# Retention in pairs of heads, and block squares added on GpSimd, in a two-layer backbone kernel

## The chip, the core and the metric

The kernel runs on one core of a Trainium2 chip. The metric is device time in microseconds (us) of one execution. The core has TensorE (matmuls into PSUM banks), VectorE, ScalarE, GpSimd and the queue of SyncE, which issues the transfers from HBM. Each engine works through its own instructions in order, and semaphores make it wait for the others.

## What is computed

Two layers act on a context of 256 tokens and an input of 256 tokens, 1024 channels each. Layer 0 mixes neighbourhood attention with a state-space scan (16 heads of 64, 2 groups) and has a dense feed-forward part; layer 1 mixes sliding-window attention with retention (8 heads) and has a mixture of eight experts. The two parts that matter here:

```python
# state space: gate, then a root-mean-square norm over each group of 512 channels
yz = (y * jax.nn.silu(z)).reshape(b, L, SSM_GROUPS, SSM_D_INNER // SSM_GROUPS)
yz = yz * lax.rsqrt(jnp.mean(jnp.square(yz), axis=-1, keepdims=True) + EPS)

# retention: decayed linear attention in both directions, then a layer norm per head
rf_c, rf_l = scan_from_context(rv_c, ga_c[0], rk_c, rq_c, rv_l, ga_l[0], rk_l, rq_l, False, need_ctx)
rb_c, rb_l = scan_from_context(rv_c, ga_c[1], rk_c, rq_c, rv_l, ga_l[1], rk_l, rq_l, True, need_ctx)
yr_l = jax.nn.silu(rgl) * head_layernorm(rf_l + rb_l, gn_g, gn_b)
```

Query and key of a retention head have 64 channels (`RET_QK_DIM`), its value 128. All arithmetic is fp32; large projections are split into a high and a low part and done as three matmuls.

## The kernel before, in words

Activations lie with channels on the 128 partitions and tokens along the row. The kernel is written stage by stage in Python; a planner takes the instructions, their dependencies and the buffers they need, and lays down for each engine an order in which an instruction written earlier goes first if it is ready. So the order of work around a line is mostly the order of the program, but whatever isn't ready in the plan is overtaken by what is written behind it. A buffer or PSUM bank is taken from a named tag; a tag has a fixed number of them ("ax", "pt" and "mm" two banks each, "po" and "ada" one; "Pm" two tiles of 128x512), and a new one waits until the old one's readers are done.

State-space stage (`ssm2`, L854 to L917). A loop goes over eight blocks `pr` of 128 channels, four to each norm group. For each block, two directions and two heads, TensorE spreads a row of decays (L877), ScalarE or VectorE turns it into a masked tile E (L882, L885, L887, L888), GpSimd scales the inputs to `xd` for three of the four combinations (L893), and TensorE multiplies (L898; the two heads go to the lower and upper 64 output partitions) and adds the off-diagonal part (L901). VectorE multiplies with the gate (L903), ScalarE squares the result into a "Pm" tile (L909), and `gsum` (L836) lets TensorE sum the squares over the partitions: four matmuls a block with a column of ones, one for each 128 tokens, all four blocks of a group into one bank. The squares of a block are summed one block later. `gdiag` and `gnorm` then build the norm. Between the blocks the output projection `out_proj` (L930) is woven in.

Retention stage (`ret`, L1213 to L1254). A loop goes over eight heads `h`. Two heads share a tile: an even head has partitions 0 to 63 of `rkT`, `rqT`, `Q` and `Hr`, an odd one 64 to 127 (`rr`). Per head: two score matmuls with 64 rows (L1220) into an "ax" bank, a multiply with the decay on VectorE (L1224), two state matmuls with 64 rows (L1228) and two with the values (L1230) into a second "ax" bank, then the layer norm: a copy (L1232), a matmul with ones for the mean (L1233), its subtraction (L1234), squares on ScalarE (L1236) and their sum by `T.matmul` with a column of ones (L1238). After heads 3 and 7 the norm of four heads is finished (L1243 to L1254) and split into `yH`, `yL`. One step of `ret` is taken after each of eight gate projections (L1257 to L1262); the output projections (L1276 and L1307) follow, and the first of them fills TensorE while retention runs. The experts' weights (L1403) are loaded into memory that retention's tiles leave.

Of the kernel before, what the change touches and what calls it, by code (L numbers as in the profile page):

```python
# [13 lines left out]
AF = mybir.ActivationFunctionType  # L14
ALU = mybir.AluOpType
# [3 lines left out]
P = 128  # L19
# [148 lines left out]
def tile_backbone(ctx: ExitStack, tc: tile.TileContext, A, out, upto=99, dbg=None):  # L168
    nc = tc.nc
    V, S, T, G = nc.vector, nc.scalar, nc.tensor, nc.gpsimd  # L170
# [25 lines left out]
    def bank(tag="mm"):  # L196
        if turn and tag == "ax":
            turn.append(turn.pop(0))
            tag = turn[0]
        return ps[0].tile([P, 512], F32, tag=tag, name="bk_" + tag, bufs=NB[tag])  # L200
# [29 lines left out]
    ident, ones = C("ident"), C("ones")  # L230
# [7 lines left out]
    def hp(shape, name, dt=F32):  # L238
        return pool[0].tile(shape, dt, tag="hp", name=name, bufs=NHP)
# [288 lines left out]
    def layer0():  # L528
# [168 lines left out]
        pt = bank("pt")  # L697
# [18 lines left out]
        pst = bank("ax")  # L716
# [13 lines left out]
        for i in range(4):  # L730
            for c in range(4):
                T.matmul(pac[32 * i:32 * i + 32, c * P:(c + 1) * P], av[:, c, :], C("tge" if i % 2 else "tle"),
                         start=True, stop=True, tile_position=(0, 32 * i))
# [10 lines left out]
        for i, m in enumerate((8, 9, 10, 11, 0, 1, 2, 3, 4, 5, 6, 7)):  # L744
# [4 lines left out]
            for d in (-2, -1, 1, 2):  # L749
# [3 lines left out]
                                       op0=ALU.mult, op1=ALU.add)  # L753
# [79 lines left out]

        psq, bks = [], []

        def gsum(pr, sq):  # L836
            for t in range(4):
                T.matmul(bks[pr // 4][:, t:t + 1], sq[:, t * P:(t + 1) * P], ones[:, 0:1],
                         start=pr % 4 == 0 and t == 0, stop=pr % 4 == 3, skip_group_check=True)

        def gdiag(g):
            return diag(rstd(bks[g][:, 0:4], 4, 1.0 / 512), 4)
# [11 lines left out]
        def ssm2():  # L854
            cbf = pg([P, 4, 2, P], "cbf")
            cbb = pg([P, 4, 2, P], "cbb")
            for g in range(2):
                pt = bank("ax")
                for c in range(4):
                    r = slice(c * P, (c + 1) * P)  # L860
                    T.matmul(pt[:, r], BT[:, g, r], CT[:, g, r], start=True, stop=True)
                ptv = pt.rearrange("p (c k) -> p c k", c=4)
                V.tensor_tensor(cbf[:, :, g, :], ptv, C("tle")[:, None, :].to_broadcast([P, 4, P]), op=ALU.mult)
                V.tensor_tensor(cbb[:, :, g, :], ptv, C("tge")[:, None, :].to_broadcast([P, 4, P]), op=ALU.mult)
            yield
            Eb = [pg([P, 2, 4, P], "E") for _ in range(5)]
            for pr in range(8):
                g = pr // 4
                py = bank("pt")
                for d in range(2):  # L870
                    Es = []
                    E2 = Eb[(2 * pr + d) % len(Eb)]
                    for hh in range(2):
                        o = d * 16 + 2 * pr + hh
                        sel = 32 * d + o
                        pt = bank("ax")
                        T.matmul(pt, idr[:, sel:sel + 1].to_broadcast([P, P]), ac2, start=True, stop=True)  # L877
                        E = E2[:, hh]
                        onact = (d, hh) in ONACT
                        for c in range(4):  # L880
                            if onact:
                                S.activation(E[:, c, :], pt[:, c * P:(c + 1) * P], AF.Relu, scale=-1.0,  # L882
                                             bias=acj[:, c, o:o + 1])
                            else:
                                V.tensor_scalar(E[:, c, :], pt[:, c * P:(c + 1) * P], lnda[:, c, o:o + 1],  # L885
                                                lndt[:, c, o:o + 1], op0=ALU.add, op1=ALU.min)
                        S.activation(E, E, AF.Exp, scale=-1.0 if onact else 1.0)  # L887
                        V.tensor_tensor(E, E, (cbb if d else cbf)[:, :, g, :], op=ALU.mult)  # L888
                        xh = [xtok[c][:, (2 * pr + hh) * 64:(2 * pr + hh + 1) * 64] for c in range(4)]
                        if onact:  # L890
                            xd = hp([P, 4, 64], "xd")
                            for c in range(4):
                                G.tensor_scalar(xd[:, c, :], xh[c], dt[:, c, o:o + 1], None, op0=ALU.mult)  # L893
                            xh = [xd[:, c, :] for c in range(4)]
                        Es.append((xh, E))
                    for c in range(4):
                        for hh in range(2):
                            T.matmul(py[hh * 64:hh * 64 + 64, c * P:(c + 1) * P], Es[hh][0][c],  # L898
                                     Es[hh][1][:, c, :], start=d == 0 and c == 0, stop=False, skip_group_check=True)
                for c in range(4):  # L900
                    T.matmul(py[:, c * P:(c + 1) * P], yo[c][:, pr * P:(pr + 1) * P], ident, start=False, stop=True,  # L901
                             skip_group_check=True)
                V.tensor_tensor(z(pr), z(pr), py, op=ALU.mult)  # L903
                if pr % 4 == 0:
                    bks.append(bank("po"))
                if psq:
                    gsum(*psq.pop())
                sq = pm_([P, 512])
                S.activation(sq, z(pr), AF.Square)  # L909
                psq.append((pr, sq))  # L910
                yield
                if pr == 4:
                    dg = gdiag(0)
                if pr == GN0:
                    gnorm(0, dg)
            gsum(*psq.pop())
            gnorm(1, gdiag(1))  # L917

        s1 = ssm1()
# [87 lines left out]
    def layer1(hH, hL):  # L1007
# [39 lines left out]
        rkT = Act(4, "rk")  # L1047
        rqT = pg([P, 4, 256], "rq")
# [21 lines left out]
        for m in range(4):  # L1070
            pp = proj(3 + m, 256)
            q = hp([P, 2, 256], "qtmp")
# [5 lines left out]
        rv = [pg([P, 1024], "rv") for _ in range(4)]  # L1078
# [3 lines left out]
        pt = bank("pt")  # L1082
# [60 lines left out]
        dec = [pg([P, 2, 2, 256], "dec") for _ in range(4)]  # L1143
# [35 lines left out]
        Q = []  # L1179
# [32 lines left out]

        def ret():  # L1213
            pst = bank("ada")
            for h in range(8):
                rr = slice((h % 2) * 64, (h % 2) * 64 + 64)
                t = h // 2
                pa = bank("ax")
                for jt in range(2):
                    T.matmul(pa[:, jt * 256:jt * 256 + 256], rkT(t, 256 + jt * P, 256 + jt * P + P)[rr],  # L1220
                             rqT[rr, t, :], start=True, stop=True)
                e = dec[h // 2][:, h % 2]
                ef = e.rearrange("p a b -> p (a b)")
                V.tensor_tensor(ef, ef, pa, op=ALU.mult)  # L1224
                bk = bank("ax")
                py, pm = bk[:, 0:256], bk[:, 256:512]
                for d in range(2):
                    T.matmul(py, Hr[rr, d, t * P:(t + 1) * P], Q[d][rr, t, :], start=d == 0, stop=False)  # L1228
                for jt in range(2):
                    T.matmul(py, rv[2 + jt][:, h * P:(h + 1) * P], e[:, jt, :], start=False, stop=jt == 1)  # L1230
                yv = yc[h // 4][:, h % 4, :]
                V.tensor_copy(yv, py)  # L1232
                T.matmul(pm, ones, yv, start=True, stop=True)  # L1233
                V.scalar_tensor_tensor(yv, pm, -1.0 / P, yv, op0=ALU.mult, op1=ALU.add)  # L1234
                sq = hp([P, 256], "sqv")
                S.activation(sq, yv, AF.Square)  # L1236
                for q in range(2):
                    T.matmul(pst[:, h * 2 + q:h * 2 + q + 1], sq[:, q * P:(q + 1) * P], ones[:, 0:1],  # L1238
                             start=h == 0 and q == 0, stop=True, skip_group_check=True)
                yield  # L1240
                if h % 4 == 3:
                    g = h // 4
                    r = rstd(pst[:, g * 8:g * 8 + 8], 8, 1.0 / P)  # L1243
                    for q in range(2):
                        pb = bank("ax")
                        diag_bcast(pb, r[:, q * 4:q * 4 + 4], 4)
                        for i in range(2):
                            hh = g * 4 + q * 2 + i
                            yv = yc[g][:, hh % 4, :]
                            V.scalar_tensor_tensor(yv, yv, vc("rgg")[:, hh:hh + 1], pb[:, i * 256:i * 256 + 256],  # L1250
                                                   op0=ALU.mult, op1=ALU.mult)
                            V.scalar_tensor_tensor(yv, yv, vc("rgb")[:, hh:hh + 1], rgs[g][:, hh % 4, :],
                                                   op0=ALU.add, op1=ALU.mult)
                            split(yH[g][:, hh % 4, :], yL[g][:, hh % 4, :], yv)  # L1254
# [681 lines left out]
    with tc.tile_pool(name="pgp", bufs=1) as pgp:  # L1936
# [3 lines left out]
        h = layer0()  # L1940
# [31 lines left out]
```

## Time and profile before

| | us |
|---|---|
| three runs | 2107.56, 2121.23, 2126.02 (median 2121.23) |
| the profiled execution | 2105.75 |
| its span from the first to the last instruction | 2103.9 |
| TensorE busy | 2035.0 |
| VectorE busy | 1284.7 |
| ScalarE busy | 905.3 |
| GpSimd busy | 102.6 |

The profile is of one execution. The busy time of TensorE is modelled for pipelined matmuls, so two matmuls in a row can overlap in it; the distance from one start to the next start is the surer reading of what a matmul costs. "PE" is TensorE's matmuls and "PEld" its weight loads, "DVE" VectorE, "ACT" ScalarE, "POOL" GpSimd, "SPq" SyncE's queue of transfers. A wait is put down to what ended it. An fp32 matmul shows as two TensorE instructions.

### The profile page before, as it was taken

Reading aid. Unit: us, or ns where it says so; the run is one execution under the profiler, and the core shown is the slowest. Engines: PE = TensorE matmul, PEld = TensorE weight load, DVE = VectorE, ACT = ScalarE, POOL = GpSimd, SP = SyncE. Lnnn points to the kernel's source line nnn. Section 1 sums busy time; section 2 is a strip of 40 time slices with the busy share of each in tenths; the row PEclk is TensorE's granted clock in tenths of the full one; section 3 lists DMA queues with packets and bytes.
Section 4 is the critical chain, followed back from the end, with each engine's and each line's share of the span. In section 5 each row is a group of like instructions: output and inputs, shape, how many; then the busy total and the mean of one; then the engine's idle time right before and its main releaser. Section 6 shows DMA issues by size and latency. Waiting matters only on the chain. (4 is left out here: it accounts for less than half of the span.)

```text
span 2103.9 us, 26774 instructions
## 1 busy us (share of the span) xinstructions
PE 2035.0 (97%) x10210; PEld 1444.8 (69%) x10210; DVE 1284.7 (61%) x1878; ACT 905.3 (43%) x1296; POOL 102.6 (5%) x143
## 2 busy tenths in 40 slices
PE   7999999989999999999999999999999999999997
PEld 4776756678777878888888888878654544545453
DVE  5366557677566664775468888898644334434543
ACT  4347515643222223544346766767532232232322
POOL 0000015500000000101101000000000000000000
PEclk9999999999999999999999999999999999999998
DMA  8423432024444673322434999999989999999984
GB/s 322 151 86 104 151 113 92 25 67 161 143 147 150 214 237 120 124 66 78 149 143 170 336 365 326 322 331 337 372 336 400 397 400 397 383 418 384 384 356 179
DMA packets 89445, 496.25 MB, mean 236 GB/s; under 512 B 10080, under 2 KB 10848, under 8 KB 46048
## 3 DMA queue, kind: packets, MB, share of 16 engines
q1 hardware_dynamic: 89312, 494.49, 64.1%
q8 instruction: 82, 1.34, 0.3%
q14 instruction: 51, 0.42, 0.1%
HBM read 493.40 MB, written 1.05 MB: 235 GB/s over the span
## 5 line engine op out<-in xcount | busy, mean ns | idle before, releaser
L270 DVE TENSOR_TENSOR w<-w 128x2048 fp32r<-128x2048 f32 (+1 forms) x186 | 384.6, 2081 | 64.1 <-ACT w L269 46.4
L269 ACT ACTIVATE w<-w 128x2048 fp32r<-128x2048 f32 (+1 forms) x186 | 320.5, 1748 | 67.7 <-DVE w L270 35.5
L269 ACT ACTIVATE whi<-raw 128x1024 fp32r<-128x1024 f32 x151 | 159.8, 1060 | 400.7 <-PE bk_mm L298 270.4
L270 DVE TENSOR_TENSOR wlo<-raw,whi 128x1024 fp32r<-128x1024 f32 x151 | 184.8, 1225 | 136.0 <-ACT whi L269 135.1
L297 PE MATMUL bk_mm<-fH,whi 128*128 128x512 f32 (+1 forms) x360 | 139.8, 390 | 2.0 <-DVE xT L518 1.1
L299 PE MATMUL bk_mm<-fH,wlo 128*128 128x512 f32 (+1 forms) x360 | 138.8, 387 | 2.1 <-DVE wlo L270 2.1
L297 PE MATMUL bk_mm<-hH,whi 128*128 128x512 f32 (+1 forms) x384 | 137.2, 360 | 3.2 <-ACT hH L269 2.2
L298 PE MATMUL bk_mm<-fL,whi 128*128 128x512 f32 (+1 forms) x360 | 139.2, 388 | 0.0
L298 PE MATMUL bk_mm<-hL,whi 128*128 128x512 f32 (+1 forms) x384 | 135.6, 354 | 0.0
L299 PE MATMUL bk_mm<-hH,wlo 128*128 128x512 f32 (+1 forms) x384 | 135.2, 353 | 0.0
L1542 PE MATMUL bk_pt<-w,xf 128*64 128x512 f32 x448 | 113.0, 601 | 0.0
L1695 ACT COPY g<-bk_ax 64x512 f32<-64x512 f32 x35 | 20.4, 582 | 207.9 <-PE bk_ax L1542 207.8
L1542 PE MATMUL bk_ax<-w,xf 128*64 128x512 f32 x448 | 107.2, 597 | 0.0
L1754 PE MATMUL bk_mm<-w,gf 128*64 128x512 f32 x448 | 105.3, 597 | 0.0
L1546 PE MATMUL bk_ax<-w,xg 128*128 128x512 f32 x224 | 91.6, 409 | 9.6 <-DVE w L270 9.6
L1545 PE MATMUL bk_ax<-w,xg 128*128 128x512 f32 x224 | 90.1, 402 | 0.0
L1547 PE MATMUL bk_ax<-w,xg 128*128 128x512 f32 x224 | 89.7, 400 | 0.0
L1546 PE MATMUL bk_pt<-w,xg 128*128 128x512 f32 x220 | 88.1, 400 | 0.4 <-DVE w L270 0.2
L1545 PE MATMUL bk_pt<-w,xg 128*128 128x512 f32 x220 | 87.6, 398 | 0.0
L1547 PE MATMUL bk_pt<-w,xg 128*128 128x512 f32 x220 | 87.3, 397 | 0.0
L297 PEld LDWEIGHTS bk_mm<-hH,whi 128*128 128x128 f32 x384 | 71.7, 188 | 22.2 <-issue 5.4
L456 POOL TENSOR_TENSOR rstd<-rstd,mhalf 128x2 f32<-128x2 f32 (+2 forms) x11 | 10.3, 937 | 1513.9 <-DVE rstd L455 1486.0
(567 smaller groups left out, 4367.4 us busy)
## 6 DMA issues: line engine op xcount, KB each, us to landing
w<-in_m SPq DMA_DIRECT2D x334, 1024.0 KB, 7.9
raw<-in_f SPq DMA_DIRECT2D x66, 512.0 KB, 3.7
araw<-in_adc SPq DMA_DIRECT2D x56, 512.0 KB, 3.9
araw<-in_ada SPq DMA_DIRECT2D x32, 512.0 KB, 7.0
raw<-in_evx SPq DMA_DIRECT2D x29, 512.0 KB, 3.8
raw<-in_odx SPq DMA_DIRECT2D x22, 512.0 KB, 3.7
raw<-in_evo SPq DMA_DIRECT2D x12, 512.0 KB, 3.6
xT<-in_xt SPq DMA_DIRECT2D x4, 1024.0 KB, 6.2
```

Source lines behind the costliest of these rows:

```text
L269: a = S.activation(hi, src, AF.Copy)
L270: v = V.tensor_tensor(lo, src, hi.bitcast(F32), op=ALU.subtract)
L297: T.matmul(o, wh, xh, start=first, stop=False)
L298: T.matmul(o, wh, xl, start=False, stop=False)
L299: T.matmul(o, wl, xh, start=False, stop=last)
L456: G.tensor_tensor(r, r, mhalf[:, :n], op=ALU.pow)
L1542: T.matmul(o[c:c + 64], sl(b[0]), wh, start=k < 2, stop=k >= K - 2, tile_position=(0, c))
L1545: T.matmul(o, sl(b[0]), wh, start=first, stop=False)
L1546: T.matmul(o, sl(b[0]), wl, start=False, stop=False)
L1547: T.matmul(o, sl(b[1]), wh, start=False, stop=last)
L1695: S.copy(g[0:64], hb[b][0][64:128])
L1754: T.matmul(accs[0][half][64 * q2:64 * q2 + 64], gT[0][0][:, f, :], wh[:, hs], start=first and q == 0, stop=last and q == 1, tile_position= ...
```

## The change

Retention takes two heads at a time. The scores of both heads are issued with the halves alternating, each head into a "pt" bank; after a new step boundary the state matmuls alternate likewise, each head in an "ax" bank; the rest of a head is as before. There are still eight steps. In the state-space stage GpSimd adds the squares of blocks 1 to 3 onto block 0, and of 5 and 6 onto block 4; TensorE sums block 0's tile alone for the first group, and for the second the tile of block 4 and that of block 7. The bank for the sums is taken when they are made.

```diff
-        def gsum(pr, sq):
+        def gsum(g, parts):
+            bks.append(bank("po"))
             for t in range(4):
-                T.matmul(bks[pr // 4][:, t:t + 1], sq[:, t * P:(t + 1) * P], ones[:, 0:1],
-                         start=pr % 4 == 0 and t == 0, stop=pr % 4 == 3, skip_group_check=True)
+                for i, sq in enumerate(parts):
+                    T.matmul(bks[g][:, t:t + 1], sq[:, t * P:(t + 1) * P], ones[:, 0:1],
+                             start=i == 0, stop=i == len(parts) - 1)
...
-                if pr % 4 == 0:
-                    bks.append(bank("po"))
-                if psq:
-                    gsum(*psq.pop())
+                if pr == 4:
+                    gsum(0, psq)
+                    psq.clear()
                 sq = pm_([P, 512])
                 S.activation(sq, z(pr), AF.Square)
-                psq.append((pr, sq))
+                if psq and pr < 7:
+                    G.tensor_tensor(psq[0], psq[0], sq, op=ALU.add)
+                else:
+                    psq.append(sq)
                 yield
...
-            gsum(*psq.pop())
+            gsum(1, psq)
             gnorm(1, gdiag(1))
...
         def ret():
             pst = bank("ada")
-            for h in range(8):
-                rr = slice((h % 2) * 64, (h % 2) * 64 + 64)
-                t = h // 2
-                pa = bank("ax")
+            for t in range(4):
+                heads = [(2 * t + i, slice(i * 64, i * 64 + 64)) for i in range(2)]
+                pa = [bank("pt") for _ in heads]
                 for jt in range(2):
-                    T.matmul(pa[:, jt * 256:jt * 256 + 256], rkT(t, 256 + jt * P, 256 + jt * P + P)[rr],
-                             rqT[rr, t, :], start=True, stop=True)
-                e = dec[h // 2][:, h % 2]
-                ef = e.rearrange("p a b -> p (a b)")
-                V.tensor_tensor(ef, ef, pa, op=ALU.mult)
-                bk = bank("ax")
-                py, pm = bk[:, 0:256], bk[:, 256:512]
+                    for (h, rr), o in zip(heads, pa):
+                        T.matmul(o[:, jt * 256:jt * 256 + 256], rkT(t, 256 + jt * P, 256 + jt * P + P)[rr],
+                                 rqT[rr, t, :], start=True, stop=True)
+                for (h, rr), o in zip(heads, pa):
+                    ef = dec[t][:, h % 2].rearrange("p a b -> p (a b)")
+                    V.tensor_tensor(ef, ef, o, op=ALU.mult)
+                yield
+                bk = [bank("ax") for _ in heads]
                 for d in range(2):
-                    T.matmul(py, Hr[rr, d, t * P:(t + 1) * P], Q[d][rr, t, :], start=d == 0, stop=False)
-                for jt in range(2):
-                    T.matmul(py, rv[2 + jt][:, h * P:(h + 1) * P], e[:, jt, :], start=False, stop=jt == 1)
...
+                    for (h, rr), o in zip(heads, bk):
+                        T.matmul(o[:, 0:256], Hr[rr, d, t * P:(t + 1) * P], Q[d][rr, t, :], start=d == 0, stop=False)
+                for (h, rr), o in zip(heads, bk):
+                    for jt in range(2):
+                        T.matmul(o[:, 0:256], rv[2 + jt][:, h * P:(h + 1) * P], dec[t][:, h % 2, jt, :],
+                                 start=False, stop=jt == 1)
+                for (h, rr), o in zip(heads, bk):
+                    yv, pm = yc[h // 4][:, h % 4, :], o[:, 256:512]
...
```

The lines of the norm that follow are those of before, inside the last loop.

## Rows read from the trace of the kernel before

**Rows 1.** The page, busy us (share of the span) x instructions, by engine:
```profile
PE 2035.0 (97%) x10210; PEld 1444.8 (69%) x10210; DVE 1284.7 (61%) x1878; ACT 905.3 (43%) x1296; POOL 102.6 (5%) x143
```
**Rows 2.** Busy by stage: stretch, its us, PE PEld DVE ACT POOL, clock, DMA, GB/s:
```profile
1020.00:1080.00 60.00, 57.32 (x340) 43.50 (x339) 29.94 (x60) 11.37 (x21) 3.27 (x2) 1.00 0.32 121
1080.00:1200.00 120.00, 118.45 (x696) 100.42 (x695) 102.60 (x190) 85.39 (x128) 6.48 (x6) 1.00 0.64 231
```
**Rows 3.** Busy by stretch, inside the state-space stage:
```profile
344.00:374.00 30.00, 28.30 (x207) 21.45 (x206) 22.05 (x42) 22.48 (x61) 26.42 (x44) 0.95 0.16 54
374.00:380.00 6.00, 4.46 (x34) 3.38 (x32) 1.17 (x3) 4.09 (x13) 1.04 (x2) 0.94 0.00 0
380.00:405.00 25.00, 23.58 (x159) 17.37 (x160) 19.73 (x38) 17.93 (x45) 21.27 (x36) 0.93 0.00 1
```
**Rows 4.** Waits of TensorE, 1020 to 1085 us: us in total, times, longest:
```profile
PE bk_ax L466 <- DVE dg L461: 2.7, 2, 1.4
```
**Rows 5.** Waits of TensorE, 335 to 420 us:
```profile
PE bk_pt L898 <- DVE E L888: 2.7, 1, 2.7
PE bk_ax L877 <- ACT E L882: 1.9, 2, 1.7
PE bk_ax L848 <- DVE dg L461: 0.4, 1, 0.4
```
**Rows 6.** Timeline of TensorE in retention: start, us, what, x instructions:
```profile
1058.80 1.13 PE L1220 MATMUL bk_ax<-rq,rk 64*128 64x256 f32 x4
1059.86 0.70 PE L1233 MATMUL bk_ax<-yc,ca 128*128 128x256 f32 x2
...
1061.08 1.13 PE L1228 MATMUL bk_ax<-qd,hr 64*128 64x256 f32 x4
1062.14 0.61 PE L1238 MATMUL bk_ada<-ca,sqv 128*128 128x1 f32 x4
```
**Rows 7.** Groups by line, TensorE, 1020 to 1080 us (busy, mean ns, idle):
```profile
L1220 PE MATMUL bk_ax<-rq,rk 64*128 64x256 f32 x32 | 9.3, 405 | 0.0
...
L1228 PE MATMUL bk_ax<-qd,hr 64*128 64x256 f32 x32 | 9.0, 402 | 0.0
```
**Rows 8.** Timeline of TensorE in the expert stage, fp32 on column halves:
```profile
1501.72 1.07 PE L1542 MATMUL bk_ax<-w,xf 128*64 128x512 f32 x2
1502.73 0.51 PE L1546 MATMUL bk_pt<-w,xg 128*128 128x512 f32 x1
...
1508.78 1.08 PE L1542 MATMUL bk_ax<-w,xf 128*64 128x512 f32 x4
1509.78 0.50 PE L1546 MATMUL bk_mm<-w,gh 128*128 128x512 f32 x1
```
**Rows 9.** Line 838, durations in ns (min/median/max), first and last start:
```profile
L838 PE MATMUL bk_po<-ca,Pm x64: 164/250/271, 351.1 to 415.3; 128*128 128x1 f32 x64
```
**Rows 10.** Timeline of TensorE, one group of the squares' sums:
```profile
407.43 1.05 PE L838 MATMUL bk_po<-ca,Pm 128*128 128x1 f32 x8
408.34 0.48 PE L297 MATMUL bk_mm<-yH,whi 128*128 128x512 f32 x1
```
**Rows 11.** Timeline of TensorE, mid-stage; in brackets the idle time before:
```profile
377.68 1.00 PE L838 MATMUL bk_po<-ca,Pm 128*128 128x1 f32 x8
381.42 0.63 PE L898 MATMUL bk_pt<-E,xtok 128*64 128x128 f32 x2 [2.74 <-DVE E L888]
```
**Rows 12.** Two GpSimd lines, durations in ns (min/median/max):
```profile
L893 POOL TENSOR_SCALAR xd<-xtok,dtp x96: 435/440/1987, 327.8 to 403.9; 128x64 f32<-128x64 f32 x96
...
L1510 POOL TENSOR_TENSOR hTok<-tmp,hTok x2: 1269/1279/1289, 1114.6 to 1115.9; 128x512 fp32r<-128x512 f32 x2
```
**Rows 13.** Waits of GpSimd, 320 to 425 us:
```profile
POOL xd L893 <- PE bk_pt L898: 12.5, 4, 8.0
```
**Rows 14.** Waits of SyncE's queue, 990 to 1130 us:
```profile
SPq L1403 <- PE bk_ax L1228: 36.1, 1, 36.1
```
**Rows 15.** Waits of TensorE, 1200 us to the end:
```profile
PE bk_ax L1546 <- DVE w L270: 14.5, 14, 2.1
```

More of the change, by code (lines that the diff above doesn't have):

```diff
@@ L1214, in ret @@
             pst = bank("ada")
-            for h in range(8):
-                rr = slice((h % 2) * 64, (h % 2) * 64 + 64)
-                t = h // 2
-                pa = bank("ax")
+            for t in range(4):
+                heads = [(2 * t + i, slice(i * 64, i * 64 + 64)) for i in range(2)]
+                pa = [bank("pt") for _ in heads]
                 for jt in range(2):
-                    T.matmul(pa[:, jt * 256:jt * 256 + 256], rkT(t, 256 + jt * P, 256 + jt * P + P)[rr],
-                             rqT[rr, t, :], start=True, stop=True)
-                e = dec[h // 2][:, h % 2]
-                ef = e.rearrange("p a b -> p (a b)")
-                V.tensor_tensor(ef, ef, pa, op=ALU.mult)
-                bk = bank("ax")
-                py, pm = bk[:, 0:256], bk[:, 256:512]
-                for d in range(2):
-                    T.matmul(py, Hr[rr, d, t * P:(t + 1) * P], Q[d][rr, t, :], start=d == 0, stop=False)
-                for jt in range(2):
-                    T.matmul(py, rv[2 + jt][:, h * P:(h + 1) * P], e[:, jt, :], start=False, stop=jt == 1)
[L1231 to L1239, printed above, removed]
@@ new lines, in ret @@
+                for (h, rr), o in zip(heads, bk):
[4 more added lines that the diff above has]
+                    yv, pm = yc[h // 4][:, h % 4, :], o[:, 256:512]
+                    V.tensor_copy(yv, o[:, 0:256])
+                    T.matmul(pm, ones, yv, start=True, stop=True)
+                    V.scalar_tensor_tensor(yv, pm, -1.0 / P, yv, op0=ALU.mult, op1=ALU.add)
+                    sq = hp([P, 256], "sqv")
+                    S.activation(sq, yv, AF.Square)
+                    for q in range(2):
+                        T.matmul(pst[:, h * 2 + q:h * 2 + q + 1], sq[:, q * P:(q + 1) * P], ones[:, 0:1],
+                                 start=h == 0 and q == 0, stop=True, skip_group_check=True)
@@ L1240, in ret @@
                 yield
+                h = 2 * t + 1
                 if h % 4 == 3:
```

## The prediction

> **What bounds the kernel now.** I read the page's engine totals first, then the busy times by stage, then who waits in the two stages that the diff touches. The totals show TensorE busy for 97% of the span and no other engine above 61% (the weight loads, 69%, are its own) [rows 1]. The reader should not trust that figure alone, because it hides stages with other limits; the table by stage tells them apart [rows 2].
>
> The retention stage (1020 to 1080 us) is TensorE's: 57.32 of 60 us, while VectorE has 29.94 and ScalarE 11.37 [rows 2]. TensorE's only listed wait there is 2.7 us for a diagonal that VectorE builds [rows 4]. Whatever retention doesn't fill, the output projection does, so a matmul that goes frees time for the next one. The stage behind it is full too: 118.45 of 120 us [rows 2]. So time saved on TensorE in retention should come out at the end.
>
> The state-space stage (about 340 to 420 us) is mixed. From 344 to 374 us TensorE has 28.30 of 30, from 380 to 405 us 23.58 of 25, and the granted clock there is 0.95 and 0.93, that is, a few stretches at the lower of its two levels (1.2 GHz) among 2.4 GHz. Between the two, from 374 to 380 us, only 4.46 of 6 us are busy [rows 3]. The named waits are 2.7 us for a masked tile E from VectorE and 1.9 us for a bank that ScalarE reads [rows 5]. In the middle blocks, then, the chain that builds E sets the pace; before and after them TensorE does.
>
> **The change part by part: retention.** Each head now issues a group of two K=64 matmuls for the scores (L1220) and, later, two for the state (L1228). An fp32 matmul is two TensorE instructions here: 32 on each line for 16 matmuls [rows 7]. One group of four runs from 1058.80 to the next start at 1059.86, thus 1.06 us, and from 1061.08 to 1062.14, again 1.06 [rows 6]. Eight heads with two groups cost 16 x 1.06 = 17.0 us. The change puts the two heads of a pair, which sit in rows 0 to 63 and 64 to 127, into one group of eight with neighbours in different halves and in different banks.
>
> No row of this trace shows row halves side by side. The nearest rows show column halves: in the expert stage a group of two instructions, which has one half alone, lasts 1502.73 - 1501.72 = 1.01 us, and a group of four that alternates the halves lasts 1509.78 - 1508.78 = 1.00 us [rows 8]. The second half is free. If rows behave like columns, eight instructions take as long as four, and 8 groups x 1.06 = 8.5 us go. If they don't, eight take twice four and nothing goes. A loss has no mechanism, since no instruction is added. Between 0 and 8.5 I go near the upper end, as the column rows are the same kind of instruction. For L1220 I take all of its 4.25 us: its operands are ready and the two "pt" banks are otherwise idle. For L1228 I take three quarters, 3.2 us, because the two "ax" banks of a pair come free one after the other, so the planner may send the first head's matmuls alone. Sum 7.4 us.
>
> The Trainium skill (TensorEngine Tiling (Array Packing), Theoretical Speedup and Key Properties) says that a contraction of at most 64 can run up to twice as fast, as tiles load and multiply independently. By it the term would be the whole 8.5 us; no run here shows it for rows yet.
>
> All the other work of a head is the same in count: four matmul instructions on rv, the mean, the squares, the reductions. Only its order moves. The pair takes four banks where a head took two, which can only shorten waits, and those on TensorE are 2.7 us in all [rows 4]. I put 0 for it. The transfers behind retention do not limit: SyncE's queue waits 36.1 us for the last L1228 before it starts the experts' weights [rows 14], so they start earlier, not later, when L1228 ends earlier.
>
> **State-space squares.** Before, each of eight blocks sends its own squares through four matmuls, 64 instructions in all, eight a group [rows 9, 10]. A group runs from 407.43 to 408.34, 0.91 us [rows 10]; eight cost 7.3. After, the first four blocks need one group (0.91), and the last four need two operands, so 16 instructions (1.8). At most 7.3 - 2.7 = 4.6 us go. But not all of them count: the group at 377.68 is followed by TensorE standing still for 2.74 us until VectorE delivers E [rows 11]. Groups ahead of that wait are covered by it; without them the wait is longer. I count only the four groups after it, less the 16 instructions that now close: 4 x 0.91 - 1.8 = 1.8 us. Bounds 0 and 4.6. The closing reduction sits 0.9 us longer ahead of the last norm; projections of the first norm group fill TensorE then, and TensorE waits 0.4 us in all for that stage's diagonals [rows 5], so 0; without that cover it costs 0.9.
>
> **GpSimd's five adds.** Blocks 1, 2, 3, 5 and 6 each get a 128x512 add on GpSimd. The nearest row is its own two-input operation of that size, 1.28 us [rows 12], thus 6.4 us. They queue in order with the 96 scalings xd, median 0.44 us, which feed the block matmuls. From 344 to 405 us GpSimd is busy 26.42 + 1.04 + 21.27 of 61 us [rows 3], so 12.3 are idle, and it waits 12.5 us for TensorE to give xd buffers back [rows 13]. An add that waits for ScalarE's Square holds up the scalings behind it, and these hold up the matmuls. With 12.3 idle for 6.4 I put 0, and for the upper bound I use the slowest row: scalings reach 1.987 us against 0.44, 4.5 times [rows 12]. Adds stretched like that take 5 x 1.28 x 4.5 = 28.8 us, 16.5 more than the idle time.
>
> The Trainium skill (GPSIMD Engine Reference, Specifications) says that GpSimd shares its SBUF interfaces with VectorE and contends with VectorE instructions that have two SBUF inputs. That is the mechanism which would stretch the adds; the spread of the scalings agrees with it, though it names no cause.
>
> **Sum.** -7.4 - 1.8 + 0 = -9.2 us. The profiled execution took 2105.75 us (span 2103.9), so it would be 2096.5. The runs shown lie at 2107.56, 2121.23 and 2126.02, so the profiled one is the quickest of four; the middle of all four is 2114.4, and I set the sum against that: **2105 us**.
>
> **The rivals.** (1) The row halves don't overlap, or the planner sends one head's matmuls together. For it speaks that no row shows them together and that the planner orders by readiness; against it stand the column halves [rows 8]. Retention then gives 0, the total is -1.8: 2112.6 us. (2) The other side: GpSimd becomes the limit of the state-space stage. It works 21.27 of 25 us late in the stage [rows 3], and its scalings already stretch. It decides once the adds take over 12.3 us together, thus 2.5 each; at 4.5 times it costs 16.5 us and the total is 16.5 - 9.2 = +7.3: 2121.7 us. Against it stands that it still waits for TensorE [rows 13]. (3) More than the sum: retention with four banks ends early, the weights start before 1071 us, and the 14.5 us which TensorE waits for VectorE's splits of expert weights [rows 15] go as well: -23.7, 2090.7 us. Against it: those waits come over the whole expert stage, long after an earlier start is used up.
>
> **How the numbers follow.** The forecast has 0.55, rival 1 0.22, rival 2 0.13, rival 3 0.10. The four runs shown spread over 20 us, 10 to each side, so the forecast's own range is 2095 to 2116. The range over all cases takes rival 3 less a few us at the low end and rival 2 at the high end: 2088 to 2123. About 1% (21 us) is what a measurement of this kernel can tell from no change. Only rival 3 passes it to the fast side, and a re-planned order elsewhere can add a little: 0.12. Rival 2 passes it only if the adds drag the clock down as well: 0.06. Within 1%: 0.82.
>
> **What would show it.** In the profile after, a group of eight on the new score line should last about 1.06 us, not 2.1, and neighbours should start within hundredths of a us; the state line shows by its groups of four or eight whether the planner kept the halves alternating. The two lines should drop from 17.0 us of TensorE's time to about 9.6. The reduction should have 24 instructions instead of 64, and the wait of 2.74 us ahead of E should grow or stay. The adds should take 1.3 to 1.7 us each, and xd should stay out of the long waits of TensorE. I would be wrong if a wait for xd grew by several us, if pairs ran one after the other, or if an order that is planned anew added stalls in a stage that the diff doesn't touch.

## The result and the profile after

| | before | after |
|---|---|---|
| 20 executions each, same chip, median, us | 2117.16 | 2100.2 |
| lowest to highest, us | 2104.58 to 2126.02 | 2095.58 to 2106.69 |
| the profiled execution, us | 2105.75 | 2096.44 |
| its span, us | 2103.9 | 2094.7 |

The ratio of the times is 0.9928, with a 95% interval of 0.991 to 0.9946. That is about 0.7% faster, inside the predicted range and 5 us under the predicted 2105.

One fact is needed to read these numbers. The executions of the kernel before fall into two groups of one length each: 9 of the 20 lie between 2104.58 and 2109.89 (mean 2106.2), 11 between 2117.11 and 2126.02 (mean 2120.5), and none between. Those of the changed kernel form one group, mean 2100.6. So the means, 2114.0 and 2100.6, differ by 13.5 us. Of these, 5.6 are the distance from the quicker group (2106.2 to 2100.6), and 11/20 x 14.4 = 7.9 come from the slower group having gone. The prediction knew one kind of gain only. Most of what follows is about the second.

The state-space stage of after, as [rows 3] (stretch, its us, PE PEld DVE ACT POOL busy, clock, DMA share, GB/s), then retention and the stage behind it, as [rows 2]:

```profile
344.00:374.00 30.00, 27.72 (x217) 20.07 (x213) 23.83 (x45) 24.39 (x69) 29.44 (x46) 1.00 0.16 54
374.00:380.00 6.00, 4.84 (x33) 4.04 (x32) 3.46 (x5) 4.37 (x13) 4.53 (x6) 0.72 0.00 1
380.00:405.00 25.00, 21.59 (x144) 14.79 (x143) 22.88 (x39) 18.55 (x46) 22.38 (x36) 0.97 0.00 1
...
1020.00:1080.00 60.00, 57.79 (x373) 47.87 (x372) 34.97 (x71) 16.94 (x31) 3.27 (x2) 0.97 0.50 193
1080.00:1200.00 120.00, 118.46 (x676) 100.44 (x675) 99.05 (x177) 85.25 (x125) 6.48 (x6) 0.99 0.61 213
```

TensorE is still the full engine behind 1020 us. From 344 to 374 us GpSimd now works 29.44 of 30 us, where it had 26.42.

The timeline of TensorE in retention of after (start, us, what, x instructions, in brackets the idle time before), as [rows 6]. The score line is L1224 here, the state line L1233:

```profile
1001.02 1.69 PE L1224 MATMUL bk_pt<-rq,rk 64*128 64x256 f32 x8 [1.72 <-DVE ktok L1196]
1002.64 0.38 PE L298 MATMUL bk_mm<-hL,whi 128*128 128x256 f32 x1
...
1007.27 1.14 PE L1224 MATMUL bk_pt<-rq,rk 64*128 64x256 f32 x8
1008.33 0.39 PE L297 MATMUL bk_mm<-hH,whi 128*128 128x256 f32 x1
...
1027.52 0.70 PE L1233 MATMUL bk_ax<-qd,hr 64*128 64x256 f32 x2
1028.14 1.97 PE L1208 MATMUL bk_ax<-rv,kd 128*64 128x128 f32 x30
...
1030.94 1.13 PE L1233 MATMUL bk_ax<-qd,hr 64*128 64x256 f32 x6
1032.00 1.99 PE L1236 MATMUL bk_ax<-dec,rv 128*128 128x256 f32 x8
...
1035.14 0.70 PE L1233 MATMUL bk_ax<-qd,hr 64*128 64x256 f32 x2
1035.76 0.61 PE L1246 MATMUL bk_ada<-ca,sqv 128*128 128x1 f32 x4
1036.30 0.70 PE L1233 MATMUL bk_ax<-qd,hr 64*128 64x256 f32 x4
1036.93 0.61 PE L1246 MATMUL bk_ada<-ca,sqv 128*128 128x1 f32 x4
1037.47 0.70 PE L1233 MATMUL bk_ax<-qd,hr 64*128 64x256 f32 x2
1038.09 3.37 PE L1236 MATMUL bk_ax<-dec,rv 128*128 128x256 f32 x8
```

Read the distance from one start to the next. Eight score instructions last 1008.33 - 1007.27 = 1.06 us, as four did before: the row halves run side by side. The state groups are cut up. The first pair goes as 2 and 6, the second as 2, 4 and 2. The reading, which e4 tests, is that a pair's two "ax" banks come free one after the other.

The waits of TensorE from 335 to 420 us of after, as [rows 5] (us in total, times, longest):

```profile
PE bk_po L840 <- POOL Pm L912: 2.5, 2, 1.3
PE bk_pt L900 <- DVE E L890: 2.3, 3, 1.1
PE bk_ax L879 <- ACT E L884: 1.2, 2, 1.0
PE bk_mm L298 <- DVE yL L270: 0.7, 1, 0.7
PE bk_ax L850 <- DVE dg L461: 0.6, 1, 0.6
```

The two waits for GpSimd's adds (L912) are new. The waits together grew from 5.0 to 7.3 us.

### The profile page after: what moved, and what is told of

It is laid out like the page before. It is cut to its first block, busy times and chain, and to the rows that moved or that the text cites. A ratio compares the mean times of both kernels' runs of the same rounds, so it can differ in the third digit from the quotient of the medians.

```text
span 2094.7 us, 26701 instructions
## 1 busy us (share of the span) xinstructions
PE 2026.0 (97%) x10170; PEld 1438.0 (69%) x10170; DVE 1288.0 (61%) x1878; ACT 906.0 (43%) x1296; POOL 109.1 (5%) x148
```

## The experiments

The theory at the start was the prediction's: the gain is TensorE time, from row halves that overlap in retention and from fewer sums of squares. Its rival: the larger part comes from the new banks and the new order of retention, whatever overlaps. Each expectation tells what its theories say of that run. The twelve runs came in three sets of four, each beside the kernel before on the same chip: 34 executions of it in the first set (11 near 2105, 23 near 2120), 35 in the second (13 and 22), 22 in the third (6 and 16). "Quick" below are a kernel's executions at a granted clock of 0.989 or more.

The last two columns are estimates, means over the quick executions. Span times granted clock is about the time that the work would take at the full clock ("work"); the rest of the span is what the lower clock took ("lost"). The clock is on record to three digits only, so differences under 1 us say nothing.

| kernel | executions | median, us | ratio to before, 95% interval | quick: count, mean us | work, us | lost, us |
|---|---|---|---|---|---|---|
| e1 squares alone | 12 | 2110.55 | 0.9979 (0.9949 to 1.0008) | 6, 2103.7 | 2086.2 | 15.8 |
| e2 pairs alone | 12 | 2105.55 | 0.9952 (0.9927 to 0.9977) | 12, 2104.6 | 2083.2 | 19.6 |
| e3 pairs, not alternating | 12 | 2104.34 | 0.9942 (0.9921 to 0.9963) | 11, 2103.5 | 2083.9 | 17.8 |
| e4 pairs, state held | 11 | 2103.42 | 0.9942 (0.9918 to 0.9967) | 11, 2102.8 | 2082.3 | 18.7 |
| e5 before again | 8 | 2119.59 | | 2, 2105.0 | 2088.5 | 14.7 |
| e6 four banks alone | 12 | 2105.72 | 0.9963 (0.9939 to 0.9988) | 12, 2105.5 | 2088.2 | 15.4 |
| e7 adds on VectorE | 12 | 2103.62 | 0.9955 (0.9931 to 0.9979) | 12, 2103.0 | 2082.5 | 18.7 |
| e8 after, state held | 12 | 2098.08 | 0.993 (0.9906 to 0.9954) | 12, 2097.2 | 2080.2 | 15.2 |
| e9 before, shift later | 10 | 2105.6 | 0.9941 (0.9913 to 0.997) | 10, 2105.1 | 2088.1 | 15.1 |
| e10 e8, shift later | 6 | 2098.78 | 0.9904 (0.9872 to 0.9936) | 6, 2099.1 | 2082.3 | 15.0 |
| e11 after again | 7 | 2102.0 | 0.9918 (0.9888 to 0.9947) | 7, 2102.4 | 2081.4 | 19.2 |
| e12 e6, shift early | 12 | 2111.08 | 0.9971 (0.9944 to 0.9998) | 10, 2110.9 | 2088.8 | 20.2 |

The kernel before's quick executions have means of 2105.2, 2105.9 and 2104.0 us in the three sets, with 2089.4, 2089.3 and 2088.5 us of work and 14.0, 14.7 and 13.7 lost. Its slower ones have 2087.1, 2087.2 and 2087.9 us of work and 30.8, 31.4 and 32.2 lost: the two groups differ by the clock. The changed kernel, in the first comparison, has 2081.4 us of work and 17.4 lost.

**e1, squares alone.** Retention is that of before; only the state-space half of the diff is in.

> The kernel before with the squares' edit alone. Theory A (the gain adds up from TensorE's time in two places): the profile after leaves the state-space stage 2.8 us earlier than before, so this kernel gains 2 to 4 us, retention is that of before, and the wait of TensorE for GpSimd's adds (5.7 us in 4 waits after) is here too. Rival B (the gain is retention's alone, and the adds' waits eat what the squares save): 0 to 1 us. Rival C (nearly all of the gain comes from here, through the clock): 10 us or more.

The quick executions fell from 2105.2 to 2103.7 and the others from 2119.7 to 2118.2. Each of these 1.5 us is uncertain by about 1.1, so they agree with the 1.8 that the prediction had for the squares, but don't show it by themselves. The two groups stay. The profiled execution was one of the slower ones, the only such profile. Its rows show where that group loses its time (columns as above):

```profile
1020.00:1056.00 36.00, 34.72 (x206) 26.18 (x202) 16.89 (x35) 7.60 (x14) 1.64 (x1) 1.00 0.33 117
1056.00:1087.00 31.00, 31.00 (x84) 21.80 (x84) 8.47 (x16) 2.19 (x4) 0.00 (x0) 0.51 0.13 45
1087.00:1120.00 33.00, 31.15 (x248) 29.12 (x247) 25.67 (x50) 20.62 (x44) 1.64 (x1) 1.00 0.53 213
```

The same stretches of the kernel before, whose profile is of a quick execution:

```profile
1020.00:1056.00 36.00, 34.72 (x218) 26.05 (x217) 18.00 (x35) 7.60 (x14) 1.64 (x1) 1.00 0.33 122
1056.00:1087.00 31.00, 29.43 (x170) 23.20 (x169) 17.86 (x39) 5.73 (x12) 1.64 (x1) 1.00 0.47 188
1087.00:1120.00 33.00, 31.62 (x241) 28.79 (x241) 25.24 (x60) 23.17 (x49) 6.48 (x6) 1.00 0.21 79
```

For 31 us TensorE is busy all the time at a granted clock of 0.51, so at 1.2 GHz, and gets through 84 instructions where the quick execution does 170. Before the fall TensorE did this (timeline of e1):

```profile
1052.45 1.13 PE L1232 MATMUL bk_ax<-qd,hr 64*128 64x256 f32 x4
...
1054.09 1.92 PE L1287 MATMUL bk_po<-rtw,mod 128*128 128x8 f32 x16
1055.86 2.06 PE L1234 MATMUL bk_ax<-dec,rv 128*128 128x256 f32 x4
1057.85 2.07 PE L1224 MATMUL bk_ax<-rq,rk 64*128 64x256 f32 x4
1059.85 1.22 PE L1237 MATMUL bk_ax<-yc,ca 128*128 128x256 f32 x2
```

The eight 8-column matmuls that make the router's shift, sixteen instructions (L1287 here, L1283 in the kernel before; "the block" from here on), are the last thing at full speed. A group of four score instructions that lasts 1.06 us [rows 6] takes 2.00 behind them. In the quick profile of the kernel before the block stands in the same place, and the clock stays at 1.00:

```profile
1056.06 1.84 PE L1283 MATMUL bk_po<-rtw,mod 128*128 128x8 f32 x16
```

So the fall comes in some executions of one and the same order.

**e2, pairs alone.** Only retention's half of the diff.

> The kernel before with retention in pairs alone. Theory A: the score groups of eight take 1.06 us, the state groups are broken up by the planner, TensorE's two lines fall from 17.1 to about 12.4 us; 4 to 8 us faster than before, and with the squares' kernel it adds up to the whole. Rival B: the whole gain, 10 to 15 us. Rival C: 0 to 2 us.

No execution near 2120 is left, so the retention stage is where the two groups come from. But the quick executions gain little: 2104.6 against 2105.2. By the estimates their work is 6.2 us less (2089.4 to 2083.2), and 5.6 of it go back as lost clock (14.0 to 19.6). In its profile, and in that of after, there are two stretches at half clock in and behind retention that the kernel before's quick profile lacks. In e2:

```profile
1040.00:1044.00 4.00, 4.00 (x15) 3.23 (x13) 1.16 (x3) 0.00 (x0) 0.00 (x0) 0.57 0.00 0
1119.00:1123.00 4.00, 4.00 (x15) 3.39 (x15) 3.79 (x17) 3.36 (x8) 0.00 (x0) 0.63 0.02 6
```

At 0.57 and 0.63 four full us lose 4 x (0.43 + 0.37) = 3.2 us of TensorE. So the profile shows where part of the 5.6 us goes; why the clock falls there is open.

**e3, the pair's matmuls in turn.** e2 with the two loops exchanged, for scores and state:

```diff
-                for jt in range(2):
-                    for (h, rr), o in zip(heads, pa):
+                for (h, rr), o in zip(heads, pa):
+                    for jt in range(2):
...
```

> Retention in pairs, with the same banks and the same steps, but each head's two matmuls are written in a row, so the row halves do not alternate; the rest is the kernel before. Theory A (row halves side by side make the gain): only one neighbour pair in a group of eight lies in different halves, the score groups take about 1.8 to 1.9 us instead of 1.06, and it is 3 to 4 us slower than the pairs that alternate. Rival (the gain comes from four banks for a pair and from the new steps, not from the halves): within 1 us of the pairs that alternate.

The expectation of 1.8 us for a group fell. A group of eight (timeline of e3) lasts 1024.14 - 1023.07 = 1.07 us:

```profile
1023.07 1.14 PE L1220 MATMUL bk_pt<-rq,rk 64*128 64x256 f32 x8
1024.14 0.38 PE L297 MATMUL bk_mm<-hH,whi 128*128 128x256 f32 x1
```

The planner left them in turn: in TensorE's queue the group is two matmuls of the lower half, then two of the upper. The eight instructions still start in four couples, 0.01 us apart within each, so the halves don't wait for each other in that order. What matters is that both heads' matmuls stand next to each other in the queue, not that they alternate.

**e4, state matmuls held.** e2, with a pair's state matmuls issued only behind the last sum of the pair before (`tail` holds that matmul), so that both banks are free:

```diff
+                with ExitStack() as es:
+                    if tail:
+                        es.enter_context(tc.issue_after(tail.pop().ins))
+                    for d in range(2):
+                        for (h, rr), o in zip(heads, bk):
...
+                tail.append(i)
```

> Retention in pairs as after, and the state matmuls of a pair are ordered behind the last sum of squares of the pair before, when both of its banks are free; the rest is the kernel before. Theory A: three of four state groups keep their alternation whole or in halves, the state line falls from 7.6 to about 5 us, and it is 1 to 3 us faster than the pairs alone, if holding them back costs nothing elsewhere. Rival (the order was as good as it gets, since what the planner pulls ahead fills waits): 0 to 3 us slower than the pairs alone.

The second and fourth pair now go as one group (timeline of e4), 1.07 us for eight where e2 and after need three groups of together 1.87:

```profile
1038.42 1.13 PE L1233 MATMUL bk_ax<-qd,hr 64*128 64x256 f32 x8
1039.49 1.78 PE L1237 MATMUL bk_ax<-dec,rv 128*128 128x256 f32 x7
```

So it was the banks that cut these groups. Two pairs save 1.6 us; the means differ by 1.7 us (2104.6 to 2102.8), less than either kernel's spread. The first and third pair stay cut.

**e5, before again.** The kernel before, unchanged, for a second profile of it.

> The kernel before, unchanged, for a second profile of it. Its executions fall into two groups, about 2105 and about 2120 us, with a mean granted clock of 0.993 and 0.985. Theory A: the slow group has one stretch of about 30 us at 1.2 GHz in retention (as the squares' kernel shows, which has the same retention); if this profile is of the slow group, it shows that stretch and retention ends 12 to 15 us later than in the first profile. Rival: the lower clock is spread over the expert stage; then retention ends where it did.

Two of eight executions were quick, and the profiled one was quick too. So the slower group's stretch was not seen in the kernel before itself.

**e6, four banks alone.** The kernel before, one head at a time, with the scores in the "pt" banks:

```diff
-                pa = bank("ax")
+                pa = bank("pt")
```

> The kernel before with the scores in the pt banks; the heads stay one at a time. It has the four banks of the pairs, but the score groups of two heads do not stand next to each other. Theory A (what pays is that two heads' 64-row matmuls stand together): the score groups still take about 1.06 us for four instructions, and the two groups of executions, 15 us apart, remain; the quick group within 2 us of that of before. Rival (the banks and the order pay): the quick group 4 to 6 us faster and no slow group, as with the pairs.

The overlap theory expected the group near 2120 to stay; it went, all twelve executions being at a clock of 0.992 to 0.994, and the quick mean stayed (2105.5 against 2105.9). A group of four score instructions still lasts 1.06 us. So the vanished group doesn't need the overlap at all. Banks change the order, and in e6 the planner puts the block at 1077.9, behind retention. That gave the theory for e9. In after the block moved too: the planner splits it (timeline of after; e2, e7 and e11 have the same split):

```profile
1045.78 1.18 PE L1292 MATMUL bk_po<-rtw,mod 128*128 128x8 f32 x10
...
1073.63 0.73 PE L1292 MATMUL bk_po<-rtw,mod 128*128 128x8 f32 x6
```

Ten instructions stand earlier than before, six behind retention. No run tests whether this alone removes the slower group from after.

**e7, adds on VectorE.** After, with one letter changed: `V.tensor_tensor` for `G.tensor_tensor`.

> The kernel after, with the five adds on VectorE instead of GpSimd. Theory (TensorE waits 5.7 us for GpSimd's adds after, so half of what the squares save is given back there): those waits go, 1 to 4 us faster than after. Rival (VectorE is 22.88 of 25 us busy late in the stage, so the adds delay the tiles E instead): 0 to 3 us slower than after.

Not faster than after (2103.0 against 2100.6 and 2102.4, both from other sets). The waits for the adds go, but others take their place (waits of TensorE in e7, 335 to 420 us):

```profile
PE bk_pt L900 <- DVE E L890: 4.4, 6, 1.1
PE bk_ax L879 <- ACT E L884: 2.0, 2, 1.5
PE bk_pt L900 <- POOL xd L895: 1.6, 1, 1.6
...
```

**e8, both halves, state held.** After, with e4's hold.

> The kernel after, with the state matmuls of a pair held behind the last sum of squares of the pair before. If the state groups are worth what their time on TensorE says: 1 to 3 us faster than after, as the held pairs against the pairs alone (2103.4 against 2105.6 us). Rival (noise of the order): within 1 us.

The best kernel of the study: mean 2097.2, 3.3 under after's 2100.6 (another set). By the estimates 1.2 of these are less work (2081.4 to 2080.2) and 2.2 less lost clock (17.4 to 15.2). The hold moves the block as well: it stands whole at 1069.1, behind retention. So these 3.3 us are not the state groups' alone.

**e9, the shift later.** The kernel before, with the block moved behind the second column block of the output projection, whose last matmul is `i`; no line of retention is touched:

```diff
-        psh = bank("po")[:, 0:8]
-        for k in range(KD):
-            T.matmul(psh, mcol(1, 1, 3, k).to_broadcast([P, P]), rtw[:, k, :], start=k == 0, stop=k == 7)
-        V.tensor_copy(shr, psh)
...
+            if m == 1:
+                psh = bank("po")[:, 0:8]
+                with tc.issue_after(i.ins):
+                    ...
+                V.tensor_copy(shr, psh)
```

> The kernel before, with one block moved: the sixteen 8-column matmuls that make the router's shift (L1283, 1.84 us) stand behind the second projection column block of the output projection instead of in the middle of retention; retention itself, its banks and its order of heads are untouched. In the profile of e1 TensorE's granted clock falls to half for 30.7 us right behind that block. Theory that the block sets off the fall: the executions around 2120 us at a granted clock of 0.983 to 0.987 are gone, the quick ones stay near 2105, so the median is 2104 to 2107, 11 to 14 us under before's. Rival, that the 64-row groups of one head at a time on the two shared banks set it off: half to two thirds of the executions stay near 2120, and the median is about 2118.

All ten executions lie between 2102.63 and 2106.92 at 0.992 to 0.994; of the kernel before beside it 16 of 22 lay near 2121.9. The quick mean is unchanged (2105.1 against 2104.0 beside it). Moving eight small matmuls takes the slower group away, with the heads' code, banks and number at a time as before. One thing changed along with it: right behind the place that the block left, the planner sends one head's state matmuls as 2 and 2 instructions with a sum between them, where the kernel before sends 4 together.

**e10 and e11, the candidate and after, side by side.** e10 is e8 with e9's move.

> The changed kernel with the state matmuls of a pair held until the previous pair's last sum (as e8), and with the router's 8-column block placed in the output projection (as e9). Theory: the block already stands behind retention in e8, so nothing is left to win: 2096 to 2099, within 2 us of e8's 2098.1, and 2 to 4 us under the changed kernel beside it (e11). Rival, that the block still costs clock where it stands: 3 us or more under e8.

> The changed kernel, unchanged, beside the others on one chip. Both theories: 2099 to 2102, all executions at a granted clock of 0.989 or more, none near 2115 to 2120.

After repeated its time (2102.0; none near 2120), and e10 is 3.2 us faster by the medians: 2097.55 to 2101.29 against 2100.81 to 2104.72. All of that is clock: by the estimates e10 loses 4.2 us less (19.2 to 15.0), and its work is no smaller (2082.3 against 2081.4). Against e8, of another set, nothing was gained, as expected.

**e12, the shift early with four banks.** e6, with the block put behind head 4's state matmuls by the same hold.

> The kernel of e6 (one head at a time, scores in four banks of their own) with the router's 8-column block put where the kernel before has it: right behind head 4's state matmuls. Theory that the block sets off the fall of the clock: part of the executions lie near 2120 at a granted clock of 0.983 to 0.987 again, and the median rises to between 2107 and 2120. Rival, that the shared banks' order does: none of the executions does, and the median is e6's 2105.7, within 1.5 us.

This came out between the two. The median rose by 5.4 us over e6, but ten of twelve executions lie at 2109.6 to 2112.8 and only two at 2117.4 and 2118.5 (clock 0.988 and 0.987). No group at 0.983 to 0.986 came back. The rise is mostly clock: over the quick executions lost time grows from 15.4 to 20.2 us, work by 0.6, which is within the estimate's error. One wait is new against e6 (waits of TensorE in e12, 1000 to 1121 us):

```profile
PE bk_mm L297 <- DVE xT L518: 1.8, 1, 1.8
```

So the long fall in the kernel before goes when the block leaves that place (e9, but for the one head's order), and the block in that place isn't enough by itself to bring it back. What else the order of the shared "ax" banks adds is open.

## Why the prediction was right, and where it was not

**The bound.** Right. TensorE's time in retention came out at the end; its last router matmul starts at 1106.63 us where it did at 1110.94, 4.3 us earlier (before, then after):

```profile
1110.94 0.29 PE L1297 MATMUL bk_ada<-rtw,xg 128*128 128x8 f32 x2
...
1106.63 0.29 PE L1306 MATMUL bk_ada<-rtw,xg 128*128 128x8 f32 x2
```

Part of a distance like this is chance: e5, the same program as before, has that matmul at 1109.5.

**Score term, -4.25 us.** Right in mechanism and nearly in size. Three groups of eight last 1.06 us, the first 1.6 with a wait inside: 4.8 us for the line instead of the 8.7 that the trace of before sums to by distances of starts, thus -3.8. The column halves [rows 8] were a fair guide to row halves. The Trainium skill (TensorEngine Tiling (Array Packing), Theoretical Speedup) gives up to a factor of two here; these groups show the whole of it.

**State term, -3.2 us: mis-sized.** The prediction named the cause, banks that come free one after the other, and still took three quarters. Pairs went as 2 and 6 (0.62 + 1.06), twice as 2, 4, 2 (1.87 each) and once as 4 and 4 (2.12), together 7.5 us instead of 8.5: -0.9. Only halves that stand in one group overlap, and a group of two costs 0.62 us, not half of 1.06. The two lines together saved 4.7 us (17.1 to 12.4), not 7.4.

**Squares, -1.8 us.** Right, a little low: in the profile of after the last matmul of the stage's output projection starts at 453.21 us instead of 455.11, -1.9, though the stage's first block matmul starts later, at 341.32 instead of 340.83. From the one to the other it is 111.9 us instead of 114.3, -2.4; e1 has 111.9 too, and e5 has 114.2. The reason was half right. The lines show 24 instructions instead of 64, 4.6 us less, and 2.3 us more waiting (5.0 to 7.3), which leaves 2.3. The wait for E did not grow ahead of one block, as forecast: it shrank to 2.3 us in three waits, and TensorE waits 2.5 us for the adds instead.

**GpSimd's adds, 0, and rival 2.** Right in the main: the waits that the adds bring are in the 2.4 us above, and they left a gain. An add takes 1.26 to 1.29 us, the row of [rows 12], not stretched:

```profile
L912 POOL TENSOR_TENSOR Pm<-Pm x5: 1262/1275/1288, 363.5 to 401.9; 128x512 f32<-128x512 f32 x5
```

Rival 2 showed itself without its price: GpSimd is full from 344 to 374 us, and TensorE waits for it twice; but with the adds on VectorE (e7) the kernel is no faster. The contention that the Trainium skill (GPSIMD Engine Reference, Specifications) states did not stretch these adds. It shows on the other engine, where the prediction did not look. VectorE's multiplies of E with the mask, two SBUF inputs, take about 0.68 us; the three that run beside an add of GpSimd take 1.18, 1.36 and 1.72 us. In the kernel before none takes over 0.80. Two rows of before, two of after, as [rows 12]:

```profile
L888 DVE TENSOR_TENSOR E<-E,cbf x16: 676/684/796, 339.8 to 404.9; 128x512 f32<-128x512 f32 x16
L888 DVE TENSOR_TENSOR E<-E,cbb x16: 676/688/724, 341.4 to 408.1; 128x512 f32<-128x512 f32 x16
...
L890 DVE TENSOR_TENSOR E<-E,cbf x16: 673/684/1715, 340.3 to 397.6; 128x512 f32<-128x512 f32 x16
L890 DVE TENSOR_TENSOR E<-E,cbb x16: 676/681/1362, 341.9 to 404.2; 128x512 f32<-128x512 f32 x16
```

In e1 the same three are long, and with the adds on VectorE (e7) none is.

**Banks and order, 0: the step that failed.** It was priced by waits alone, 2.7 us [rows 4]. Its true worth is the 7.9 us of the mean that the slower executions cost, since banks alone (e6) or the block's place alone (e9) take that group away. No wait shows that: in the slower execution TensorE is busy 31.00 of 31 us, at half the clock. The text took the spread of 20 us over four executions for noise, though its own table had two times near 2106 and two above 2121 and only the quick kind was profiled. The granted clock over a whole span, 0.991 or more against 0.987 or less in the kernel before's executions of the three sets, tells the two kinds apart.

**The sum.** -9.2 us was set against a middle of 2114.4, where no execution of the kernel before lies. For a quick execution the change gives 5.6 us in the first comparison, and 1.6 where after was repeated (2104.0 to 2102.4). In that repeat the estimates give 7.1 us less work (2088.5 to 2081.4), as much as the lines do (4.7 and 2.4), and 5.5 us more lost clock (13.7 to 19.2). So most of the forecast's work was there, less what the cut state groups kept, and the clock took most of it back. Part of that is new stretches at half clock: from 1039 to 1043 and from 1117 to 1121 us after's clock is 0.63 and 0.57, as e2's. The profiled pair differs by 9.3 us, as forecast, but not for the forecast's reason. Beyond the 4.3 us at the router 5 more come in the expert stage, which the change doesn't touch. There the kernel before's profile fell to half clock twice and after's did not, which makes up for the two new stretches. Before and after:

```profile
1500.00:1600.00 100.00, 96.48 (x405) 51.99 (x405) 44.98 (x48) 30.18 (x31) 0.00 (x0) 0.98 0.90 356
1950.00:2050.00 100.00, 96.96 (x426) 51.60 (x424) 46.71 (x60) 29.88 (x34) 0.00 (x0) 0.98 0.92 367
```

```profile
1490.00:1590.00 100.00, 96.47 (x411) 54.27 (x411) 48.93 (x48) 33.84 (x33) 0.00 (x0) 1.00 0.91 359
1940.00:2040.00 100.00, 96.97 (x434) 50.92 (x432) 46.84 (x59) 30.72 (x35) 0.00 (x0) 1.00 0.93 370
```

That the time came out at 2100 is thus a smaller gain in work than predicted and a gain in clock that was not. That the number fell inside the range is in part luck.

**Rivals 1 and 3.** Rival 1 fell with the first group of eight in 1.06 us; its second half, a planner that takes the heads apart, held for the state. Rival 3's place is right in part: SyncE's queue waits 13.9 us instead of 36.1 for the state line [rows 14], but TensorE's waits for splits of expert weights only went from 14.5 [rows 15] to 12.1 us.

## What to carry to other kernels

Look at single times and at the granted clock of each before pricing a change: a spread in two groups can be a mechanism, and a profile shows only one of them. Span times granted clock parts work from clock. Work with 64 rows that can stand next to its neighbour in the other half of the array costs half, if its banks come free together; where they don't, holding the group until they do brings the overlap back (e4), though that this shortened the kernel was not shown apart from the clock. A block of very narrow matmuls can be worth moving even where TensorE is never idle. Adds moved to GpSimd can keep their time and still stretch what VectorE runs beside them.

## What the chip showed that was not expected

- TensorE can run at 1.2 GHz while it is busy without a gap: 31 us at 0.51 in e1, from right behind eight 8-column matmuls. The Trainium skill (TensorE: Matmul & The Clock Gate, HAM oscillation) tells of falls behind idle gaps; the last one here was a wait of 1.3 us, 9 us before the fall. What triggers it, beyond that it went when the block was moved, is open.
- Row halves overlap with no alternation in the code or the queue: 1.07 us for eight instructions in turn (e3), 1.06 alternating.
- VectorE's two-input multiplies take 1.18 to 1.72 us beside GpSimd's two-input adds and about 0.68 else, while the adds keep their 1.26 to 1.29.
- Four state instructions, two in each half, take 0.63 us, as two of one half do (0.62).
